# Block copies of the output weights on GpSimd's queue, each transfer tied to a weight split

## The chip, the cores and the metric

The kernel runs on one core of one Trainium2 chip. The metric is the device time of one execution in microseconds (us); lower is better. A core has TensorE (PE, matrix products), VectorE (DVE), ScalarE (ACT) and GpSimd (POOL), each with its own queue of instructions that runs strictly in order, and SyncE (SP), which here only starts transfers. Transfers run on 16 DMA engines that all queues share. A transfer that SP starts goes through hardware queue q1, one that GpSimd starts through software queue q0.

## The reference

One encoder layer on 512 tokens of width 2048, in float32: a normalised, modulated input, one wide input projection, two mixers that read it (dilated-window attention with 16 heads, and gated linear attention, GLA, with 4 heads in both directions), a SiLU gate on each, one output projection, and a normalised residual sum.

```python
mod = jax.nn.silu(c) @ w_cond[layer] + b_cond[layer]
shift, scale, gate = jnp.split(mod, 3, axis=-1)
h = rms_norm(x) * (1.0 + scale[:, None]) + shift[:, None]
proj = h @ w_in[layer]
aq, ak, av, ag, gq, gk, gv, gg, lr_f, lr_b = jnp.split(proj, PROJ_SPLITS, axis=-1)
...
a_out = att.reshape(B, S, ATT_WIDTH) * jax.nn.silu(ag)
...
g_out = g_o * jax.nn.silu(gg)
y = jnp.concatenate([a_out, g_out], axis=-1) @ w_out[layer]
x = x + gate[:, None] * y
return rms_norm(x) * final_gain
```

## The kernel before

**Products.** Each float32 operand is split into a high part (rounded by ScalarE, `split_hi`, L438) and a low part (the difference, by VectorE, `split_lo`, L424), and each product is three TensorE products of such parts (`three`, L215 to L217).

**Stages.** First the modulation (`cb` loads, sums on VectorE) and the first projections (`sta`, `stb`). Then ten units, in this order: qk2, qk4, qk6, gk, gv0, gv1, ag0, ag1, gg0, gg1. A unit (`unit`) makes 512 columns of the projection in eight groups; a group loads 512 KB of weights (`raw`, four buffers, on SP), splits them (three buffers for each part), and does 24 matmuls of 512 columns. At the start of group g the program asks for the split of group g + 1, and it fetches two groups further ahead. Between a unit's matmuls the program puts side work at fractions of its 64 ticks: attention in the first four units, GLA heads in gv1 to gg0, and from qk6 on sums for the gate and the value bias, whose `rawv` and `rawg` loads share the four `raw` buffers and whose work is VectorE's (L314, L839).

**Attention.** For each tile: scores on TensorE (`s`, L726 and L727), a minimum on VectorE (L730), an exponential on ScalarE (L733), a reciprocal on VectorE (`st`, L734), a scaling on GpSimd (`p`, L738), four transposes on TensorE (`t`, L750), a split of the result (`pt`, L754 and L755), and the product with the values (`o`, L764). Between two units the keys of the next four heads are evicted and copied to the other half of the partitions by small SP transfers (`ks`, `kl`). In qk6 the row `srow` and then its spread copy `shb` are also stored and loaded on SP; VectorE's first `rawv` sum needs them. In a GLA head, VectorE's state updates (`st`) take turns with a scaling on GpSimd (`dc`, L926), and `z` (L865) is the head's first product; it needs `lrst` and `ups`, made by VectorE at the start of gv1.

**Output projection.** It is done in two column pairs, each with seven block products in place of eight (`OUT_ORDER`), so some weight operands are sums of blocks: T1 = 11 + 12, T3 = 12 + 22, T2 = T1 + 22, T4 = T2 + 21, four row groups each, for two pairs. That makes 32 sums of 512 KB. Each is made in DRAM, long before the output stage, by two transfers: `sum_start` copies the first block into a DRAM tile (on SP, L393), and `sum_add` adds the second to it in the transfer (on GpSimd, L399). `sum_ops` lists these 64 steps in order, and `SUM_OPS_IN` says how many of them each unit takes; a unit spreads its n steps at fractions (q + 0.5) / n of its ticks.

**Order.** TensorE's order is the program's. On the other engines a scheduler orders the instructions by data dependences and priorities. `tc.issue_after` keeps a transfer behind a named instruction in the order of its own queue: a copy behind SP's last weight load, an addition behind GpSimd's last `p`.

Of the kernel before, what the change touches and what calls it, by code (L numbers as in the profile page):

```python
# [13 lines left out]
AF = mybir.ActivationFunctionType  # L14
ALU = mybir.AluOpType
# [104 lines left out]
OUT_WEIGHTS = {"P1": "11", "P7": "T3", "P6": "T2", "P4": "T4", "P5": "T1", "P3": "22", "P2": "21"}  # L120
OUT_SUMS = {"T1": ("11", "12"), "T3": ("12", "22"), "T2": ("T1", "22"), "T4": ("T2", "21")}
OUT_DEEP = 6
SUM_OPS_IN = {"qk2": 7, "qk4": 7, "qk6": 7, "gk": 7, "gv0": 5, "gv1": 7, "ag0": 7, "ag1": 6, "gg0": 6, "gg1": 5}


def _plan(tasks, free, ready):
# [52 lines left out]
def block_kernel(ctx: ExitStack, tc: tile.TileContext, a: dict):  # L179
    nc = tc.nc  # L180
# [27 lines left out]
    act = nc.scalar.activation  # L208
# [36 lines left out]
    def RAW(name, shape):  # L245
        return wp.tile([P] + shape, F32, tag="raw", bufs=4, name=name)
# [103 lines left out]
    raws, wts, low, last = {}, {}, set(), {}  # L350

    def fetch(i):
        if i < len(groups) and i not in raws:
            u, g = groups[i]
            if u == "O":
                raws[i] = out_fetch(g)
            else:
                raws[i] = RAW(f"raw_{u}{g}", [2, 512])
                last["load"] = nc.sync.dma_start(raws[i], a["w_" + u][g]).ins

    def out_block(pair, which, g):

        l, r = OUT_PAIRS[pair]
        j, z = {"11": (l, g), "21": (l, 4 + g), "12": (r, g), "22": (r, 4 + g)}[which]
        return a[f"w_o{j}"][z]

    def out_fetch(s):

        pair, q = divmod(s, 4 * len(OUT_ORDER))
        what, g = OUT_WEIGHTS[OUT_ORDER[q // 4]], q % 4  # L370
        if s % 2 and s >= OUT_DEEP:
            t = op.tile([P, 2, 512], F32, tag="raw", bufs=3, name=f"raw_O{s}")
        else:
            t = RAW(f"raw_O{s}", [2, 512])
        if what in OUT_SUMS:
            d = dsum[pair, what, g]
            nc.sync.dma_start(t.rearrange("p k c -> p (k c)"),
                              bass.AP(d.tensor, d.offset, [[1024, P], [1, 1024]]))
        else:
            nc.sync.dma_start(t, out_block(pair, what, g))  # L380
        return t

    dsum = {}

    def flat(t):
        return bass.AP(t.tensor, t.offset, [[2048, 64], [1, 2048]])

    def sum_start(pair, name, g):
        def go():
            src = OUT_SUMS[name][0]  # L390
            dsum[pair, name, g] = t = dp.tile([64, 2048], F32, tag=f"{name}{pair}{g}", name=f"{name}{pair}{g}")
            with tc.issue_after(last["load"]):
                nc.sync.dma_start(t, flat(dsum[pair, src, g] if src in OUT_SUMS else out_block(pair, src, g)))  # L393
        return go

    def sum_add(pair, name, g):
        def go():
            with tc.issue_after(last["pool"]) if "pool" in last else nullcontext():
                nc.gpsimd.dma_start(dsum[pair, name, g], flat(out_block(pair, OUT_SUMS[name][1], g)),  # L399
                                    accum_op=ALU.add, max_dma_last_dim=8192)  # L400
        return go

    sum_ops = []
    for s in range(13):
        for lag, fn, name in ((0, sum_start, "T1"), (0, sum_start, "T3"), (1, sum_add, "T1"), (1, sum_add, "T3"),
                              (2, sum_start, "T2"), (3, sum_add, "T2"), (4, sum_start, "T4"), (5, sum_add, "T4")):
            if 0 <= s - lag < 8:
                sum_ops.append(fn(*[((s - lag) // 4), name, (s - lag) % 4]))

    def block_sums(name):  # L410
        n = SUM_OPS_IN[name]
        r = [sum_ops.pop(0) for _ in range(n)]
        return [((q + 0.5) / n, x) for q, x in enumerate(r)]

    def split(i):
        split_hi(i)
        split_lo(i)
# [9 lines left out]
    def split_hi(i):  # L427
        if i < len(groups) and i not in wts:
            fetch(i)
            u, g = groups[i]  # L430
            raw = raws[i].rearrange("p k c -> p (k c)")
            dst = None
            if (u, g) == ("O", len(groups) - gi["O", 0] - 4):
                t = b8.tile([P, 2, 1024], F32R, tag="b8", name="wlast")
                dst = t[:, 0, :], t[:, 1, :]
            wts[i] = dst or (wp.tile([P, 1024], F32R, tag="whi", name=f"{u}{g}h"),
                             wp.tile([P, 1024], F32R, tag="wlo", name=f"{u}{g}l"))
            act(wts[i][0], raw, AF.Copy)  # L438

# [179 lines left out]
    for z in range(2):  # L621
        for e in range(3):
            name = ("mm", "a", 0, 7) if (z, e) == (1, 2) else ("m0", z, e)
# [28 lines left out]
    for w in range(4):  # L652
        for kt in range(4):
            j, g = w // 2 * 4 + kt, w % 2
            task(("vh", j, g), "ACT", 0.42, ["rcol", ("vo", j), ("vl", j - 1, g) if kt else ("hi", 4 * w + 3)],
                 300 - 4 * w - kt, lambda j=j, g=g: v_high(j, g), None if kt else "b8")
            task(("vl", j, g), "DVE", 0.44, [("vh", j, g)], 300 - 4 * w - kt, lambda j=j, g=g: v_low(j, g))
    task(("f", 0), "DMA", 1.5, [("w", "b", KT - 1)], 10, lambda: fetch(0), "raw")
    task(("f", 1), "DMA", 1.5, [("f", 0)], 9, lambda: fetch(1), "raw")
    for i in range(2):  # L660
        task(("s", i), "DVE", 1.3, [("f", i), ("wl", "b", KT - 1)], 850, lambda i=i: split(i), "wts", "raw")
# [341 lines left out]
    def unit(name, natural, side=(), lr=None):  # L1003
# [5 lines left out]
        for g in range(KT // 2):  # L1009
            i0 = gi[name, g]  # L1010
            split_hi(i0)
            split_hi(i0 + 1)
            for ahead in (2, 3):
                fetch(i0 + ahead)
            split_lo(i0)
            hi, lo = wts[i0]
            for i in range(4):
                for kk in range(2):
                    k = 2 * g + kk
                    rh, rl = h_hi[:, k, :], h_lo[:, k, :]  # L1020
                    if natural:
                        t = slice(i * P, i * P + P)
                        cw = slice(kk * 512, kk * 512 + 512)
                        three(ps[i], rh[:, t], rl[:, t], hi[:, cw], lo[:, cw], k == 0, k == KT - 1)
                    else:
                        c = slice(kk * 512 + i * P, kk * 512 + i * P + P)
                        three(ps[i], hi[:, c], lo[:, c], rh, rl, k == 0, k == KT - 1)
                    tick += 1
                    if tick % 8 == 2:
                        split_lo(i0 + 1)  # L1030
                    while pos < len(side) and side[pos][0] * ticks <= tick:
                        urgent(side[pos][1])
                        pos += 1
                if lr is not None:
                    lr(4 * g + i)
# [123 lines left out]
    for e in "hl":  # L1159
        t = hp.tile([P, KT, 512], F32R, tag="h", name="c_" + e)  # L1160
# [263 lines left out]
```

## Time and profile before

| what | us |
|---|---|
| median of 3 runs | 941.84 |
| lowest and highest | 941.41, 942.56 |
| the profiled execution, its time | 948.97 |
| its span, first to last instruction | 947.2 |
| VectorE, ScalarE busy in it | 655.3, 472.8 |
| GpSimd's transfers of sums (L399), median to landing | 7.8 |
| SP's copies from the weights (L393), median to landing | 6.0 |
| rawv loads, rawg loads, median to landing | 4.8, 4.4 |

The times of all rows below the second come from one profiled execution, which took 7.1 us longer than the median. How to read the views that follow: a row of the timeline or of the chain has the start and the length in us, then engine, line, operation and tiles; "x7" after it counts merged instructions, and brackets hold the idle time just before and what ended it. A row of waits has the total in us, the number and the longest. A row of windows has the stretch, its length, the busy time of PE, PEld (weight loads), DVE, ACT and POOL with the number of instructions in parentheses, then the granted TensorE clock, the share of time in which the DMA engines were busy, and GB/s. A queue's row has packets, MB and the share of 16 engines' span.

### The profile page before, as it was taken

To read this page: it belongs to the slowest core of one execution; us is meant where nothing else is said; L and a number is where in the kernel's file an instruction comes from. 1 tells how busy PE (TensorE), PEld (TensorE's weight loads), DVE (VectorE), ACT (ScalarE), POOL (GpSimd) and SP (SyncE) were. 2 spreads that over 40 slices of the span, in tenths; PEclk is the share of its full clock that TensorE was granted. 3 is DMA by queue.
4 is the path that set the end of the run, shared out by engine and by line. 5 is a ranking of instruction groups with operands and counts; after the bars stand their busy time and mean duration, and the time that the engine had idled before them with its cause. 6 is when DMAs were issued, how large, how long until landed. Compare 5 with 4: busy or idle time off the path is not lost.

```text
span 947.2 us, 12118 instructions
## 1 busy us (share of the span) xinstructions
PE 920.3 (97%) x4375; PEld 762.4 (80%) x4375; DVE 655.3 (69%) x960; ACT 472.8 (50%) x770; POOL 84.3 (9%) x120
## 2 busy tenths in 40 slices
PE   8999999999999999999899899999999999999996
PEld 6888888888888878888677688888878888888884
DVE  7988899775756666776333747567697629697486
ACT  5553533655555645555312436354464428555464
POOL 0000000012122122123000010101001000000001
PEclk9999999999999999999899999999999999999998
DMA  9999496654663674954856847566666556866743
GB/s 350 404 411 377 184 374 238 222 156 148 169 203 107 175 260 155 261 177 127 236 156 223 229 157 204 160 218 223 222 217 204 181 153 244 315 210 216 280 176 136
DMA packets 52803, 209.79 MB, mean 221 GB/s; under 512 B 7204, under 2 KB 7492, under 8 KB 45960
## 3 DMA queue, kind: packets, MB, share of 16 engines
q1 hardware_dynamic: 49680, 191.61, 56.5%
q0 software_dynamic: 2624, 16.84, 9.8%
q8 instruction: 34, 0.56, 0.2%
q10 hardware_dynamic: 440, 0.57, 0.2%
q14 instruction: 25, 0.20, 0.1%
HBM read 200.53 MB, written 37.83 MB: 252 GB/s over the span
## 4 chain that ended last, share of the span: by engine, by line
PE 79%; DMA 10%; DVE 5%; issue 3%; ACT 2%; ACTq 0%; DVEq 0%; SPq 0%
DMA rawv<-in_wv 5%; PE ps_qk L215 4%; PE ps_qk L216 4%; PE ps_qk L217 4%; PE g L217 4%; PE g L215 4%; PE g L216 4%; PE stb L217 3%; PE stb L216 3%; PE stb L215 3%; PE ps_ag L217 3%; PE ps_ag L215 3%; PE ps_ag L216 3%; PE t L750 3%; PE o L764 3%
## 5 line engine op out<-in xcount | busy, mean ns | idle before, releaser
L733 ACT ACTIVATE p<-p,st 128x512 f32<-128x512 f32 x64 | 46.1, 720 | 57.7 <-DVE st L730 57.2
L314 DVE CUSTOM_DVE_ANT_0 cb<-cb,sb,c_bcond 128x2048 f32<-128x2048 f32 (+1 forms) x32 | 73.5, 2296 | 0.9 <-DMA cb<-in_wm 0.9
L738 POOL TENSOR_SCALAR p<-p,st 128x512 f32<-128x512 f32 x62 | 44.1, 711 | 327.9 <-DVE st L734 280.1
L730 DVE CUSTOM_DVE_ANT_0 p<-s,g 128x512 f32<-128x512 f32 x64 | 43.7, 688 | 17.8 <-PE s L727 17.2
L755 DVE TENSOR_TENSOR pt<-t,pt 128x512 fp32r<-128x512 f32 x64 | 43.7, 689 | 16.7 <-ACT pt L754 16.2
L399 POOL DMA_DIRECT2D T<-in_w_o x32 | 25.2, 981 | 241.5 <-DMA T<-T 181.4
L754 ACT ACTIVATE pt<-t 128x512 fp32r<-128x512 f32 x64 | 37.9, 592 | 10.7 <-PE t L750 9.7
L764 PEld LDWEIGHTS o<-pt,vv 128*128 128x128 f32 x256 | 35.4, 193 | 7.4 <-DVE pt L755 4.6
L764 PE MATMUL o<-pt,vv 128*128 128x256 f32 x256 | 36.4, 286 | 4.2 <-DVE pt L755 4.2
L750 PEld LDWEIGHTS t<-c_ident,p 128*128 128x128 f32 x256 | 31.8, 141 | 9.9 <-POOL p L738 1.4
L750 PE MATMUL t<-c_ident,p 128*128 128x128 f32 x256 | 39.0, 275 | 0.1
L314 DVE CUSTOM_DVE_ANT_0 rawg<-rawg,sb,gate 128x1024 f32<-128x1024 f32 x16 | 20.5, 1281 | 24.4 <-DMA rawg<-in_wg 24.4
L726 PE MATMUL s<-ks,qs 128*128 128x512 f32 x64 | 25.5, 398 | 1.9 <-DVE pt L755 1.9
L734 DVE RECIPROCAL st<-st 128x1 f32<-128x1 f32 x64 | 10.3, 161 | 24.6 <-ACT p L733 24.5
L314 DVE CUSTOM_DVE_ANT_0 rawg<-rawg,sb,c_bcond 128x1024 f32<-128x1024 f32 x16 | 20.5, 1280 | 7.7 <-DMA rawg<-in_wg 7.7
L727 PE MATMUL s<-kl,qs 128*128 128x512 f32 x64 | 25.2, 394 | 0.0
L314 DVE CUSTOM_DVE_ANT_0 rawv<-rawv,shb,vbias 128x1024 f32<-128x1024 f32 x8 | 10.3, 1282 | 21.3 <-DMA rawv<-in_wv 21.3
L839 DVE CUSTOM_DVE_ANT_0 rawv<-rawv,shb 128x1024 f32<-128x1024 f32 x8 | 9.8, 1223 | 21.0 <-DMA rawv<-in_wv 18.2
L767 ACT ACTIVATE oh<-o 64x256 f32<-64x256 f32 x32 | 12.2, 382 | 19.8 <-PE o L764 19.0
L933 ACT ACTIVATE sq<-st,sc 128x256 f32<-128x256 f32 x24 | 12.2, 507 | 17.4 <-DVE st L928 9.4
L771 DVE TENSOR_TENSOR cat<-o,oh 64x256 f32<-64x256 f32 x32 | 13.3, 416 | 9.1 <-ACT oh L767 8.7
L1249 POOL TENSOR_SCALAR x<-x,rn 128x512 f32<-128x512 f32 x3 | 3.4, 1139 | 178.4 <-ACT rn L1238 178.4
(1519 smaller groups left out, 2973.3 us busy)
## 6 DMA issues: line engine op xcount, KB each, us to landing
cb<-in_wm SPq DMA_DIRECT2D x31, 1024.0 KB, 8.9
T<-in_w_o POOLq DMA_DIRECT2D x32, 512.0 KB, 7.8
rawg<-in_wg SPq DMA_DIRECT2D x32, 512.0 KB, 4.4
raw_O<-T SPq DMA_DIRECT2D x32, 512.0 KB, 4.5
raw_qk<-in_w_qk SPq DMA_DIRECT2D x24, 512.0 KB, 3.4
raw_O<-in_w_o SPq DMA_DIRECT2D x24, 512.0 KB, 4.3
rawb<-in_w_sb SPq DMA_DIRECT2D x16, 512.0 KB, 5.5
T<-in_w_o SPq DMA_DIRECT2D x16, 512.0 KB, 6.0
```

Of the source, the lines that this page charges most:

```text
L215: mm(ps, lh, rh, start=first, stop=False, skip_group_check=more)
L216: mm(ps, ll, rh, start=False, stop=False, skip_group_check=more)
L217: mm(ps, lh, rl, start=False, stop=last, skip_group_check=more)
L314: nc.vector.tensor_tensor_reduce(out=w, in0=w, in1=with_, op0=ALU.mult, op1=ALU.add, scale=1.0, scalar=init, accum_out=dst)
L726: mm(ps, qs[:, q], ks, start=True, stop=False)
L730: nc.vector.tensor_tensor_reduce(out=t, in0=ps, in1=gt[h][:, P * i:P * i + 512], op0=ALU.add, op1=ALU.min, scale=1.0, scalar=3e38, accum_o ...
L733: act(t, t, AF.Exp, bias=st[:, 0:1], scale=-1.0, accum_out=st[:, 1:2])
L738: last["pool"] = nc.gpsimd.tensor_scalar(t, t, st[:, 2:3], 1.0, op0=ALU.mult, op1=ALU.mult).ins
L750: nc.tensor.transpose(pk[:, kt * P:kt * P + P], t[:, kt * P:kt * P + P], ident)
L754: act(hi, src, AF.Copy)
L755: tt(lo, src, hi.bitcast(F32), op=ALU.subtract)
L764: mm(po[:, :256], vv[h // 4][:, kt, h % 4, :], t[:, w, kt, :], start=kt == 0 and w == 0, stop=kt == 3 and w == 1)
```

## The change

`sum_start` no longer uses SP. Both steps go through a new function, `paced`: a GpSimd transfer in pieces of 8 KB that stays behind GpSimd's last `p`, and that also waits, by a semaphore, for the latest weight split that the program has asked of ScalarE. `last["load"]` falls away. The first units take more steps (qk2 and qk4 nine each instead of seven), the units qk6 to gv1 fewer (6, 6, 4, 5 instead of 7, 7, 5, 7), ag1 seven instead of six; the sum stays 64.

```diff
-SUM_OPS_IN = {"qk2": 7, "qk4": 7, "qk6": 7, "gk": 7, "gv0": 5, "gv1": 7, "ag0": 7, "ag1": 6, "gg0": 6, "gg1": 5}
+SUM_OPS_IN = {"qk2": 9, "qk4": 9, "qk6": 6, "gk": 6, "gv0": 4, "gv1": 5, "ag0": 7, "ag1": 7, "gg0": 6, "gg1": 5}
...
-                last["load"] = nc.sync.dma_start(raws[i], a["w_" + u][g]).ins
+                nc.sync.dma_start(raws[i], a["w_" + u][g])
...
+    def paced(dst, src, **how):
+
+        with tc.issue_after(last["pool"]) if "pool" in last else nullcontext():
+            move = nc.gpsimd.dma_start(dst, src, max_dma_last_dim=8192, **how).ins
+        tc.add_manual_dep(move, last["hi"].name, mybir.DependencyInfo(
+            mybir.DependencyClass.Sync, mybir.DependencyReason.DATA), reason="paced")
+
     def sum_start(pair, name, g):
         def go():
             src = OUT_SUMS[name][0]
             dsum[pair, name, g] = t = dp.tile([64, 2048], F32, tag=f"{name}{pair}{g}", name=f"{name}{pair}{g}")
-            with tc.issue_after(last["load"]):
-                nc.sync.dma_start(t, flat(dsum[pair, src, g] if src in OUT_SUMS else out_block(pair, src, g)))
+            paced(t, flat(dsum[pair, src, g] if src in OUT_SUMS else out_block(pair, src, g)))
         return go
 
     def sum_add(pair, name, g):
         def go():
-            with tc.issue_after(last["pool"]) if "pool" in last else nullcontext():
-                nc.gpsimd.dma_start(dsum[pair, name, g], flat(out_block(pair, OUT_SUMS[name][1], g)),
-                                    accum_op=ALU.add, max_dma_last_dim=8192)
+            paced(dsum[pair, name, g], flat(out_block(pair, OUT_SUMS[name][1], g)), accum_op=ALU.add)
         return go
...
-            act(wts[i][0], raw, AF.Copy)
+            last["hi"] = act(wts[i][0], raw, AF.Copy).ins
```

GpSimd's queue at the end of attention, before: the last two p (heads 15) and what follows them. T and three digits is a DRAM sum: name, pair, group; a row from in_w_o with no addition mark can be a copy or an addition, and a second row for the same T is its addition.

```order
L738 TENSOR_SCALAR p150_3963<-p150_3963,st150_3964 128x512
L738 TENSOR_SCALAR p151_4009<-p151_4009,st151_4010 128x512
L399 DMA T110_3148<-in_w_o2 64x2048
L399 DMA T310_3259<-in_w_o2 64x2048
L399 DMA T202_3555<-in_w_o1 64x2048
L399 DMA T400_3709<-in_w_o0 64x2048
L399 DMA T111_3819<-in_w_o2 64x2048
L399 DMA T311_3930<-in_w_o2 64x2048
L399 DMA T203_4208<-in_w_o1 64x2048
```

The same place in the change, with the waits of each:

```order
L742 TENSOR_SCALAR p150_3965<-p150_3965,st150_3966 128x512 [waits DMAHW2_49,DMAHW3_49,DVE_49,PE_49]
L391 DMA T203_4000<-T103_2318 64x2048 [waits DMASW6_49]
L742 TENSOR_SCALAR p151_4013<-p151_4013,st151_4014 128x512 [waits DMAHW4_49,DVE_49,PE_49]
L391 DMA T202_3216<-in_w_o1 64x2048 [waits DMASW7_49]
L391 DMA T401_4214<-T201_2637 64x2048 [waits DMASW0_49,Activation_49]
L391 DMA T400_3446<-in_w_o0 64x2048 [waits DMASW1_49,Activation_49]
L391 DMA T112_4365<-in_w_o3 64x2048 [waits DMASW2_49,Activation_49]
L391 DMA T312_4446<-in_w_o2 64x2048 [waits DMASW3_49,Activation_49]
```

Of the seven additions behind the last p only T202 stays there; those of T110 and T310 have moved ahead into attention, and the transfers behind T202 wait for ScalarE (Activation) as well.

GpSimd's queue in ag0, in the change, around the two directions of one GLA head (dc10 and dc11):

```order
L391 DMA T112_4365<-in_w_o2 64x2048 [waits DMASW4_49,Activation_49]
L930 TENSOR_SCALAR dc101_5121<-st100_5116,sc10_4942 128x256 [waits DVE_49,Pool_49]
L930 TENSOR_SCALAR dc102_5126<-st101_5120,sc10_4942 128x256 [waits DVE_49]
L391 DMA T312_4446<-in_w_o2 64x2048 [waits DMASW5_49,Activation_49]
L930 TENSOR_SCALAR dc111_5169<-st110_5164,sc11_4971 128x256 [waits DVE_49,Activation_49,Pool_49]
```

Before, the transfer at this place was T211's addition, which waited for its copy; now it is T312's, which waits for its copy and for a split of ScalarE.

GpSimd's queue at the end of unit qk4 (the last p of head 7, then the first of head 8), in the change:

```order
L742 TENSOR_SCALAR p72_2691<-p72_2691,st72_2692 128x512 [waits DVE_49]
L391 DMA T200_2263<-in_w_o1 64x2048 [waits DMASW4_49]
L742 TENSOR_SCALAR p73_2733<-p73_2733,st73_2734 128x512 [waits DVE_49,PE_49]
L391 DMA T110_2794<-in_w_o3 64x2048 [waits DMASW3_49]
L391 DMA T310_2893<-in_w_o2 64x2048
L742 TENSOR_SCALAR p80_2913<-p80_2913,st80_2914 128x512 [waits DVE_49,PE_49]
```

Before, the additions of T102 and T302 stood between p73 and p80, and the copy T201 stood on SP ahead of the keys ks of head 8; now two copies stand between the p, one addition ahead of p73, and none of them on SP.

## The prediction

> **What bounds the kernel now.** The page first, for the share of each engine; then TensorE's windows of 25 us, for where the rest is lost.
>
> ```profile
> span 947.2 us, 12118 instructions
> PE 920.3 (97%) x4375; PEld 762.4 (80%) x4375; DVE 655.3 (69%) x960; ACT 472.8 (50%) x770; POOL 84.3 (9%) x120
> ```
> ```profile
> 325.00:350.00 25.00, 23.07 (x109) 18.91 (x108) 15.39 (x35) 10.43 (x21) 4.88 (x7) 0.93 0.80 248
> 450.00:475.00 25.00, 20.77 (x94) 16.92 (x93) 8.18 (x14) 8.17 (x16) 0.00 (x0) 0.86 0.86 226
> 500.00:525.00 25.00, 23.65 (x104) 18.46 (x103) 8.45 (x11) 6.17 (x8) 1.55 (x2) 1.00 0.74 231
> 525.00:550.00 25.00, 21.47 (x91) 17.40 (x90) 19.50 (x23) 14.00 (x25) 0.77 (x1) 0.93 0.64 184
> 825.00:850.00 25.00, 25.00 (x112) 20.71 (x111) 21.20 (x28) 13.25 (x19) 0.00 (x0) 1.00 0.66 230
> ```
> TensorE is full in a window such as the last. So only its few holes can be won, and every new hole is paid in full. TensorE's own waits name the holes:
>
> ```profile
> PE o L764 <- DVE pt L755: 4.2, 1, 4.2
> PE z L865 <- DVE ups L1098: 3.5, 1, 3.5
> PE s L726 <- DVE pt L755: 1.9, 1, 1.9
> PE kt L904 <- DVE ki L894: 1.6, 1, 1.6
> PE ps_gv L217 <- DVE gv06l L424: 1.4, 1, 1.4
> PE ps_gv L217 <- DVE gv05l L424: 0.3, 1, 0.3
> ```
> Together 12.9 us. Behind three of them the granted clock drops (0.93, 0.86, 0.93 above), and TensorE's timeline shows the price at the largest:
>
> ```profile
> 457.90 2.07 PE L764 MATMUL o<-pt,vv 128*128 128x256 f32 x8 [4.20 <-DVE pt L755]
> 459.77 0.63 PE L215 MATMUL ps_gk<-h_hi,gk7h 128*128 128x512 f32 x1
> 462.33 0.45 PE L215 MATMUL ps_gk<-h_hi,gk7h 128*128 128x512 f32 x1
> 463.08 0.40 PE L215 MATMUL ps_gv<-gv00h,h_hi 128*128 128x512 f32 x1
> 463.31 0.39 PE L216 MATMUL ps_gv<-gv00h,h_lo 128*128 128x512 f32 x1
> ```
> Six matmuls from 459.77 to 462.33 start 0.43 us apart instead of 0.23: 1.2 lost, and the eight of L764, half as wide, take 1.87 to the next start instead of 8 x 0.115: 0.9 lost. So 2.1 us there. The windows at 325 and 525 lose 0.07 of the clock where that at 450 loses 0.14; between half of 2.1 and all of it I put 1.5 each. Holes and clock together: 12.9 + 2.1 + 3.0 = 18.0 us, the most that can be won.
>
> **Why the largest hole is there.** GpSimd's queue, and the chain of waits with VectorE's timeline beside it:
>
> ```profile
> 443.81 5.62 POOL L399 DMA_DIRECT2D T<-in_w_o  x7
> ```
> ```profile
> 446.06 9.75 DMA rawv<-in_wv
> 457.27 10.40 DMA rawv<-in_wv
> 470.20 4.20 DMA rawv<-in_wv
> 514.86 9.93 DMA rawg<-in_wg
> ```
> ```profile
> 455.94 1.28 DVE L314 CUSTOM_DVE_ANT_0 rawv<-rawv,shb,vbias 128x1024 f32<-128x1024 f32 x1 [5.23 <-DMA rawv<-in_wv]
> 524.92 1.29 DVE L314 CUSTOM_DVE_ANT_0 rawg<-rawg,sb,gate 128x1024 f32<-128x1024 f32 x1 [10.09 <-DMA rawg<-in_wg]
> ```
> Seven additions leave in one burst at 443.81. The two rawv loads that meet them take 9.75 and 10.40 us, the next one 4.20. VectorE works in order: it sits at the late load, with the pt that TensorE wants queued behind it. In gv0 each rawv load also waits for a buffer that VectorE frees, so the lateness is carried on to gv05l and gv06l.
>
> **The change part by part.** (1) 32 copies leave SP's queue for GpSimd's. No TensorE hole waits for an SP issue, so SP gains nothing that counts. GpSimd pays one issue each, as its additions do:
>
> ```profile
> 273.71 0.70 POOL L738 TENSOR_SCALAR p<-p,st 128x512 f32<-128x512 f32 x1 [1.03 <-DVE st L734]
> 274.35 0.77 POOL L399 DMA_DIRECT2D T<-in_w_o  x1
> 401.09 1.40 POOL L738 TENSOR_SCALAR p<-p,st 128x512 f32<-128x512 f32 x2 [15.12 <-DVE st L734]
> ```
> 32 x 0.77 = 25 us on an engine that is busy 84 us. In the order of the change one transfer at most stands between two p of a unit, in gaps of which the shortest concerned is the 1.03 us above, and pairs stand only at unit ends, in gaps like the 15.12: hidden. Without that cover it would be 0.8 us a time.
>
> (2) The engine time of a copy and of an addition:
>
> ```profile
> q1 hardware_dynamic: 49680, 191.61, 56.5%
> q0 software_dynamic: 2624, 16.84, 9.8%
> ```
> q0 carries the 32 additions: 0.098 x 947.2 = 93 us of all 16 engines, 2.9 us each. At q1's rate (0.565 x 947.2 = 535 us for 191.6 MB) a copy of 0.52 MB is 1.5 us. A copy in 8 KB pieces on q0 is not in this trace: between 1.5 and 2.9; I take 1.5, since it does no addition. So the total load stays, and what counts is whom it meets.
>
> (3) The pace. In the order of the change only one addition (T202) follows the last p that GpSimd does; the next four transfers belong to gv0 and wait for the splits of gv01, gv03, gv05 and gv07, two groups or at least 2 x 24 x 0.23 = 11 us of TensorE work apart. The load of 446.06 then meets one addition instead of seven: 5 to 6 us instead of 9.75, and VectorE is through some 4.5 us sooner. **Hole at 453: 6.3 (4.2 + 2.1); I take 5.5**, bounds 3 and 6.3. **gv05l and gv06l: 1.7; I take 1.5**, bounds 0 and 1.7.
>
> (4) z at 530.75 waits behind the rawg load of 514.86 (9.93 us), which meets two copies and two additions. Now:
>
> ```profile
> 510.61 1.06 ACT L438 ACTIVATE gv11h<-raw_gv 128x1024 fp32r<-128x1024 f32 x1 [7.44 <-PE ps_gv L216]
> 513.61 1.22 DVE L424 TENSOR_TENSOR gv11l<-raw_gv,gv11h 128x1024 fp32r<-128x1024 f32 x1
> ```
> The first addition of gv1 is let go by the end of gv11h, and the rawg load starts when gv11l has freed its buffer: the two still meet, but one to one. Estimate for the load 7 us, and its issue is earlier against TensorE by what gv0 no longer loses. **5.0 (3.5 + 1.5); I take 3.5**, bounds 0 and 5.0.
>
> (5) The hole at 337 (s L726):
>
> ```profile
> 314.51 0.48 SPq L393 DMA_DIRECT2D T<-T  x1
> 314.94 1.59 POOL L399 DMA_DIRECT2D T<-in_w_o  x2
> ```
> ```profile
> 317.66 8.19 DMA ks<-ks
> 325.91 5.93 DMA srow<-shiftt
> 331.90 4.52 DMA shb<-srow
> ```
> ```profile
> 336.45 1.23 DVE L839 CUSTOM_DVE_ANT_0 rawv<-rawv,shb 128x1024 f32<-128x1024 f32 x1 [2.79 <-DMA shb<-srow]
> ```
> A copy and two additions (1.5 + 2 x 2.9 = 7.3 us) lie ahead of ks; srow starts when ks has landed. Now one addition goes out some 4 us earlier, before the last p of qk4, and two copies (3.0) take this place. **3.4 (1.9 + 1.5); I take 3.0**, bounds 0 and 3.4.
>
> (6) kt at 708.5 hangs on a long row of VectorE work, whose order the change shifts by an instruction or two: 1.6 at most either way; I take 0.5.
>
> (7) Against it: at the end of qk2 two additions now leave together after p33, ahead of the next ks. A hole like that of 337 would cost 3.4; the ks and the first score share GpSimd's gap of some 15 us there, so it is mostly hidden: I take 1.0 lost. For GpSimd's new waits 0.5.
>
> **Sum:** 5.5 + 1.5 + 3.5 + 3.0 + 0.5 - 1.5 = 12.5 us of this execution, which took 948.97. The median is 941.84, 7.1 less. If all of that is holes, the median has 11 of the 18 left; if none, all 18. I take the middle, 0.8: 12.5 x 0.8 = 10.0, so **931.8 us**; its own range is 926 to 938.
>
> **Rivals.** *Slower: turn-taking.* A copy on SP's queue waits behind the load ahead of it; on q0 it runs beside the loads, and q0's pieces stretch them, as 9.75 against 4.20 shows. Place: ks at three unit ends, and rawv and rawg in gv0 and gv1, where VectorE has no slack. If two more unit ends become like 337 (6.8), and the five copies of gv0 and gv1 each stretch a load by half of what the burst did (5.55 / 2 x 5 = 13.9), less the burst (6.3), 14.4 us are lost: 956 in full, 949 at half. It decides from where ks takes over 8 us, as at 317.66. For it: q0 is now active about 93 + 48 us. Against it: a copy is half an addition, and additions that met loads singly left no hole in most windows. The Trainium skill, "DMA: Bandwidth & Descriptors" (Queues, rings and completion order), says that each engine goes round robin between queue rows, a packet at a time; by that rule this rival's mechanism is real, and the loads above agree, with its size left to the rows.
>
> *Slower: GpSimd stuck.* It is in order too, and a transfer that waits for a split now stands between two dc:
>
> ```profile
> 602.11 1.04 ACT L438 ACTIVATE ag06h<-raw_ag 128x1024 fp32r<-128x1024 f32 x1
> 606.08 0.48 POOL L926 TENSOR_SCALAR dc<-st,sc 128x256 f32<-128x256 f32 x1 [1.75 <-DVE st L923]
> ```
> ag06h ends at 603.15, plus 0.8 for the issue, and dc comes at 606.08: 2.1 us spare. A split later than that holds dc, VectorE's next st and all splits behind. Five such places at 2 us: 952.
>
> *Half a gain.* Only the burst goes, and the other holes come from VectorE's own loop of load, sum and split: 0.8 x 6.3 = 5.0, 936.8.
>
> *No effect.* In attention the order shows hardly a wait on ScalarE at the transfers, so the pace is not enforced there; gains and new holes cancel: 942.
>
> **How the numbers follow.** Forecast 0.55, half a gain 0.17, no effect 0.08, turn-taking 0.14, stuck 0.06. The range goes from all 18 won (923.8) to turn-taking at a little over a fifth of its price: 924 to 945. Under 0.2% (1.9 us) a measurement here does not tell a change from none: faster 0.74, same 0.07, slower 0.19.
>
> **What would show it.** Right: no run of seven on GpSimd near 444, the rawv loads after 444 under 7 us, no hole at o L764, granted clock 1.00 from 450 to 475. Step 4: rawg ahead of z under 8 us. Step 5: ks at 317 under 6 us. Wrong: a ks or kl over 8 us after qk2 or qk6 with a hole at s; dc waiting for DMA or for a split; p on GpSimd ending after TensorE wants its t.

## The result, and the profile after

| kernel | median, us | lowest to highest | runs |
|---|---|---|---|
| before | 942.89 | 939.03 to 948.34 | 20 |
| changed | 942.64 | 938.62 to 947.34 | 20 |

The ratio is 0.9994, with a 95% interval of 0.9977 to 1.0011: no difference that can be measured. The forecast of 931.8 us was wrong. The profiled execution of the changed kernel took 940.34 us. Its page, with the span, the engines and the two queues:

```profile
span 938.6 us, 12129 instructions
PE 917.5 (98%) x4375; PEld 760.8 (81%) x4375; DVE 654.6 (70%) x960; ACT 472.2 (50%) x770; POOL 98.3 (10%) x152
q1 hardware_dynamic: 48656, 174.83, 51.1%
q0 software_dynamic: 5184, 33.62, 15.1%
```

The copies are on q0 now: it carries twice the bytes, and 0.151 x 938.6 = 142 us of all engines where it had 93. The 49 us more are 1.5 us for each of the 32 copies, as step (2) took.

GpSimd's timeline where the burst of seven additions was, and VectorE's waits for loads in the whole span:

```profile
441.04 0.78 POOL L391 DMA_DIRECT2D T<-in_w_o  x1
447.01 0.53 POOL L391 DMA_DIRECT2D T<-T  x1 [5.19 <-ACT gv01h L442]
461.50 0.77 POOL L391 DMA_DIRECT2D T<-in_w_o  x1 [13.97 <-ACT gv03h L442]
473.36 0.53 POOL L391 DMA_DIRECT2D T<-in_w_o  x1 [11.08 <-ACT gv05h L442]
```
```profile
DVE rawg L314 <- DMA rawg<-in_wg: 50.0, 18, 5.7
DVE rawv L843 <- DMA rawv<-in_wv: 16.0, 7, 6.0
DVE rawv L314 <- DMA rawv<-in_wv: 15.0, 6, 4.6
```

One transfer leaves at a time, and from gv0 on each is let go by a split. No wait for a rawv load is over 6.0 us. From issue to landing the longest rawv load between 444 and 485 takes 5.8 us, the rawg load at 501.5, ahead of the first z, 5.5, and the ks at 318 4.8. TensorE's windows (columns as before) and its largest waits after the first stages show what that brought and what came in its place:

```profile
325.00:350.00 25.00, 25.00 (x129) 20.97 (x128) 16.50 (x37) 12.36 (x25) 6.35 (x9) 1.00 0.72 241
450.00:475.00 25.00, 25.00 (x118) 20.45 (x118) 9.71 (x14) 7.47 (x11) 1.30 (x2) 1.00 0.60 195
525.00:550.00 25.00, 25.00 (x137) 21.54 (x136) 13.77 (x19) 10.26 (x20) 3.25 (x6) 1.00 0.40 128
600.00:625.00 25.00, 22.10 (x112) 18.59 (x111) 13.54 (x20) 12.36 (x17) 2.07 (x3) 0.93 0.67 198
675.00:700.00 25.00, 21.86 (x97) 17.78 (x96) 21.23 (x28) 13.60 (x25) 1.84 (x3) 0.96 0.69 224
```
```profile
PE kt L908 <- DVE ki L898: 3.1, 1, 3.1
PE z L869 <- DVE cat L992: 2.9, 1, 2.9
PE s L730 <- DVE cat L775: 0.2, 1, 0.2
```

The first three windows are full at clock 1.00: the holes at s, o and z that the prediction priced are gone, and every sign that it named for being right is there. All of these signs lie ahead of ag0. The last two, in ag1 and gg0, have new holes. How one of them arises can be read in the chain of waits, in GpSimd's timeline, in VectorE's and in TensorE's:

```profile
603.12 7.43 DMA rawg<-in_wg
610.61 1.18 issue
611.89 5.68 DMA rawg<-in_wg
617.71 1.28 DVE rawg L314
619.00 1.32 DVE cat L992 x2
```
```profile
600.92 0.78 POOL L391 DMA_DIRECT2D T<-in_w_o  x1 [6.70 <-ACT ag10h L442]
610.84 0.53 POOL L391 DMA_DIRECT2D T<-T  x1 [9.15 <-ACT ag11h L442]
```
```profile
610.57 1.28 DVE L314 CUSTOM_DVE_ANT_0 rawg<-rawg,sb,c_bcond 128x1024 f32<-128x1024 f32 x1 [3.19 <-DMA rawg<-in_wg]
617.71 1.28 DVE L314 CUSTOM_DVE_ANT_0 rawg<-rawg,sb,gate 128x1024 f32<-128x1024 f32 x1 [4.70 <-DMA rawg<-in_wg]
```
```profile
616.52 0.39 PE L217 MATMUL ps_ag<-h_lo,ag10h 128*128 128x512 f32 x1
619.81 0.76 PE L869 MATMUL z<-lrst,ups 128*128 128x512 f32 x1 [2.90 <-DVE cat L992]
620.37 0.63 PE L215 MATMUL ps_ag<-h_hi,ag10h 128*128 128x512 f32 x1
620.80 0.63 PE L216 MATMUL ps_ag<-h_hi,ag10l 128*128 128x512 f32 x1
```

Each of the two rawg loads meets a transfer that a split has let go, 2.2 us before the first load and 1.1 before the second. VectorE idles 3.19 and 4.70 us at them, `cat` is queued behind, and TensorE's z waits for `cat`. Behind the hole the matmuls start 0.43 us apart instead of 0.23, so the hole costs more than its 2.90. The hole at kt in gg0 has another shape: the rawg load in its chain takes 4.18 us, as short as the 4.20 of the load that met no burst before.

Where the time went is best read from the start of each unit's first matmul in TensorE's timeline:

| profiled execution | ag0 starts | gg1 starts | ag0 to gg1 | rest |
|---|---|---|---|---|
| before | 577.4 | 741.4 | 164.0 | 205.8 |
| before, a second one | 574.2 | 737.1 | 162.9 | 205.7 |
| changed | 561.1 | 732.8 | 171.7 | 205.8 |
| changed, one from a later run | 560.2 | 736.9 | 176.7 | 205.8 |

The changed kernel reaches ag0 between 13 and 17 us earlier. From there to gg1 it takes 8 to 14 us more than before. How many differs from execution to execution, which fits the spread of the runs over some 9 us.

### The profile page after: what moved, and what is told of

It is laid out like the page before. It is cut to its first block, busy times and chain, and to the rows that moved or that the text cites. A ratio compares the mean times of both kernels' runs of the same rounds, so it can differ in the third digit from the quotient of the medians.

```text
span 938.6 us, 12129 instructions
## 1 busy us (share of the span) xinstructions
PE 917.5 (98%) x4375; PEld 760.8 (81%) x4375; DVE 654.6 (70%) x960; ACT 472.2 (50%) x770; POOL 98.3 (10%) x152
## 4 chain that ended last, share of the span: by engine, by line
PE 81%; DMA 8%; DVE 7%; issue 3%; ACT 1%; POOL 0%; SPq 0%; DVEq 0%; POOLq 0%; ACTq 0%
DMA rawg<-in_wg 5%; PE ps_qk L215 4%; PE ps_qk L217 4%; PE ps_qk L216 4%; PE g L217 4%; PE g L215 4%; PE g L216 4%; PE stb L217 3%; PE stb L216 3%; PE stb L215 3%; PE o L768 3%; PE ps_gv L217 3%; PE ps_gv L216 3%; PE ps_gv L215 3%; PE t L754 3%
## 5 line engine op out<-in xcount | busy, mean ns | idle before, releaser
L391 POOL DMA_DIRECT2D T<-in_w_o x48 | 33.5, 704 | 311.3 <-ACT qk21h L442 119.8
L314 DVE CUSTOM_DVE_ANT_0 rawg<-rawg,sb,gate 128x1024 f32<-128x1024 f32 x16 | 20.5, 1283 | 31.1 <-DMA rawg<-in_wg 30.9
L314 DVE CUSTOM_DVE_ANT_0 rawg<-rawg,sb,c_bcond 128x1024 f32<-128x1024 f32 x16 | 20.5, 1282 | 19.1 <-DMA rawg<-in_wg 19.0
```

The source lines that it names most:

```text
L314: nc.vector.tensor_tensor_reduce(out=w, in0=w, in1=with_, op0=ALU.mult, op1=ALU.add, scale=1.0, scalar=init, accum_out=dst)
L391: move = nc.gpsimd.dma_start(dst, src, max_dma_last_dim=8192, **how).ins
```

## The experiments

All times stand beside runs of the kernel before on the same chip. Ratios are to these, with a 95% interval. The chip differs between experiments, so the ratios compare better than the times.

**The two kernels once more, unchanged.**

> The kernel before, unchanged, profiled once more. Theory 'unlucky profile' (the profiled execution of 948.97 us was a slow draw from a spread of 939 to 948, and its 12.8 us of holes are more than the usual): other or smaller holes than at 337, 453 and 527, together 5 to 9 us, and a profiled time near 942. Theory 'given back' (the change takes these holes away in every execution and makes as many in ag1 and gg0): the same three holes, 11 us or more together, and a gv0 and gv1 of 112 to 114 us together. Ratio to before 1.000 either way.

> The changed kernel, unchanged, profiled once more. 'Given back': holes in front of z (ag1) and of kt (gg0) again, 2.5 to 3.5 us each, and none at s, o or in gv0. 'Unlucky profile': its profile of 940.34 us was a fast draw, so this one shows more holes, 9 us or more, some of them in attention or gv0, and a time near 943.

> The changed kernel, unchanged, timed and profiled once more beside the others of this call. 'No net effect' (the 20 runs so far): ratio 0.998 to 1.002. 'Given back' with a real rest won (its two profiles took 940.3 and 939.9, those of before 949.0 and 944.6): ratio 0.993 to 0.997. Holes in front of z in ag1 and kt in gg0, each 2.5 to 3.5 us, in both cases.

Before: 945.17 us, ratio to itself 0.999 (0.9973 to 1.0006). Changed: one execution at 939.89, and then 942.47, ratio 0.9966 (0.9949 to 0.9984). So the change is worth between nothing and 0.5%, and the bound of a measurement of this kind is about 0.2%. The second trace of before has the same three holes, but smaller: 4.3 us at o, 3.1 at z and 1.5 at s, 8.9 together where 11 or more were expected. The changed kernel's has 3.3 us at z and 2.5 at kt again, and only 0.8 at o. The holes are thus those of the kernels, and not of one execution.

**No sums at all** (the kernel before; the output stage loads a plain block in place of each sum).

```diff
         def go():
-            src = OUT_SUMS[name][0]
...
+            pass
```

> The kernel before without the 64 transfers that make the sums; the output stage loads a plain block where it would load a sum, so the output is not the reference's. It gives the most that any rearrangement of these transfers can win. 'Given back': they cost holes of about 12 us in both kernels, so 930 to 933 us. 'Unlucky profile': holes come mostly from VectorE's own loop of loads and sums, so 937 to 941 us.

930.03 us, ratio 0.9833 (0.9811 to 0.9855). The 64 transfers cost the kernel before some 16 us, and no arrangement tried here won more; the prediction's 18.0 was near it.

**The queue without the pace** (the changed kernel).

```diff
-        tc.add_manual_dep(move, last["hi"].name, mybir.DependencyInfo(
-            mybir.DependencyClass.Sync, mybir.DependencyReason.DATA), reason="paced")
```

> The changed kernel without the wait for the split: copies and additions both on GpSimd's queue in 8 KB pieces, new numbers per unit. 'Given back': if the pace is what empties gv0, a burst on GpSimd behind the last p returns, a hole of 3 to 4 us near 453, and 944 to 950 us. 'Unlucky profile': no difference that can be measured, 941 to 944 us.

969.13 us, ratio 1.0241 (1.0218 to 1.0265). TensorE's waits in it:

```profile
PE ps_gv L217 <- DVE gv04l L426: 8.5, 1, 8.5
PE ps_gv L217 <- DVE gv05l L426: 6.4, 1, 6.4
PE o L766 <- DVE pt L757: 4.8, 1, 4.8
```

When the attention is over nothing holds GpSimd back: it sends one transfer after the other, gv0 takes 76.9 us in place of 52.3, and ag0 to gg0 behind it run as without sums (54.1, 54.1 and 55.3). So without the pace the move of the copies is a plain loss, well above the 944 to 950 us that I expected.

**The same transfers, but small** (the changed kernel; each transfer moves 64 x 32 numbers in place of 64 x 2048, and the output stage loads plain blocks).

```diff
-        return bass.AP(t.tensor, t.offset, [[2048, 64], [1, 2048]])
+        return bass.AP(t.tensor, t.offset, [[2048, 64], [1, 32]])
```

> The changed kernel with the same instructions, waits and order on VectorE, ScalarE and GpSimd, but each of the 64 transfers moves 64 x 32 numbers in place of 64 x 2048, and the output stage loads plain blocks: the sums are left out. If the holes in front of z (ag1) and kt (gg0) come from the bytes that meet the rawg loads, they are gone and the time is that without sums, 930 us (929 to 932). If they come from the other order on VectorE, or from GpSimd waiting for splits, both holes stay and the time is 935 to 940 us.

930.79 us, ratio 0.9849 (0.9827 to 0.9871), as without sums. Behind the first stages TensorE has one wait of note left:

```profile
PE kt L905 <- DVE ki L895: 1.1, 1, 1.1
```

The instructions of the four engines up to the output stage, the waits on GpSimd and the numbers per unit are those of the change. So neither GpSimd's issues nor its waits for splits nor VectorE's order cost anything that can be measured; the holes in ag1 and gg0 come from the bytes.

**Still more steps in the first units** (the changed kernel).

```diff
-SUM_OPS_IN = {"qk2": 9, "qk4": 9, "qk6": 6, "gk": 6, "gv0": 4, "gv1": 5, "ag0": 7, "ag1": 7, "gg0": 6, "gg1": 5}
+SUM_OPS_IN = {"qk2": 11, "qk4": 11, "qk6": 9, "gk": 9, "gv0": 4, "gv1": 4, "ag0": 6, "ag1": 3, "gg0": 2, "gg1": 5}
```

> The changed kernel with other numbers per unit: qk2 11, qk4 11, qk6 9, gk 9, gv0 4, gv1 4, ag0 6, ag1 3, gg0 2, gg1 5; the order on the other engines stays. If the two late holes come from transfers that meet rawg loads, they shrink to under 1 us each and the time is 934 to 938 us, unless the denser transfers of attention make new holes in front of s or o (rival: 942 to 946 us). If they come from VectorE's order, they stay and the time is that of the changed kernel within 2 us.

948.11 us, ratio 1.0028 (1.0009 to 1.0046). TensorE's waits:

```profile
PE ps_gk L215 <- DVE kl L704: 5.5, 1, 5.5
PE kt L908 <- DVE ki L898: 2.7, 2, 2.5
PE s L730 <- DVE pt L759: 2.5, 1, 2.5
PE o L768 <- DVE pt L759: 1.5, 1, 1.5
```

Attention cannot take the transfers of ag1 and gg0: new holes at s, at the start of gk and at o cost more than is won, and the time is above both of the ranges that I expected. Nor is the number of transfers all that counts: with six of them started in ag1 and gg0 instead of 13, kt in gg0 still waits 2.5 us.

**The numbers alone** (the kernel before with the new `SUM_OPS_IN`, copies on SP and additions without a wait).

> The kernel before with the changed numbers per unit and nothing else: copies on SP, additions not paced. If the numbers win the gain in gv0 and gv1, the hole in front of o near 452 is under 2 us and the time 3 to 6 us under before. If it is the pace, GpSimd still sends a burst of additions behind its last p, the hole stays at 3 to 5 us, and the time is within 2 us of before.

938.77 us, ratio 0.9926 (0.9905 to 0.9948): one line of the change does better than the whole of it. The hole at o remains, as GpSimd's timeline and TensorE's waits say:

```profile
439.73 4.82 POOL L399 DMA_DIRECT2D T<-in_w_o  x6
```
```profile
PE o L764 <- DVE pt L755: 4.4, 1, 4.4
```

**Queue and pace with the old numbers** (the fourth corner; the changed kernel with the old `SUM_OPS_IN`).

> Queue and pace of the change with the old numbers per unit: the fourth corner beside the kernel before, the changed kernel and the kernel with the new numbers alone (938.8, 7 us under the kernel before). If the parts add up, queue and pace cost 4 us by themselves: about 949. If the pace does the same work as the numbers at the hole at 453 (it breaks up the burst of additions), the hole at o is gone here too and the time is within 2 us of the changed kernel, so that the loss lies in ag1 and gg0 alone: about 943.

944.27 us, ratio 0.9978 (0.9966 to 0.999). The wait at o falls to 1.2 us in its trace, so queue and pace break the burst up without the numbers; but s waits 3.1 us. Against the kernel before, queue and pace together win next to nothing; against the numbers alone they lose.

**The old way from ag0 on** (the changed kernel; the last 25 steps as before, copies on SP, additions without a wait).

```diff
+        late = len(sum_ops) >= 39
...
-            paced(t, flat(dsum[pair, src, g] if src in OUT_SUMS else out_block(pair, src, g)))
+            if late:
+                with tc.issue_after(last["load"]):
+                    nc.sync.dma_start(t, flat(dsum[pair, src, g] if src in OUT_SUMS else out_block(pair, src, g)))
+            else:
+                paced(t, flat(dsum[pair, src, g] if src in OUT_SUMS else out_block(pair, src, g)))
```

> The changed kernel up to the end of gv1 (39 transfers); the 25 transfers of ag0 to gg1 go the old way, copies on SP behind its last weight load, additions on GpSimd without the wait for a split. Theory A (a paced transfer is let go by the very split that frees the raw buffer for the next rawg load, so transfer and load meet one to one in ag0 to gg1): the change keeps its gain up to gv1 (gv1 starts near 506) and ag1 and gg0 lose their holes at z and kt; ag1 falls from 58.7 us to about 55 and gg0 from 58.9 to about 55.5, so 5 to 8 us under the changed kernel, about 935 where the kernel before is at 943 to 946. Theory C (any 25 transfers in these units cost about the same, whoever starts them): ag1 and gg0 stay within 1.5 us of the changed kernel, and the time too.

934.08 us (932.91 to 934.68), ratio 0.9873 (0.9858 to 0.9888). ag1 and gg0 take 54.1 and 55.5 us in its trace, against 58.7 and 58.9 in the changed kernel's. The same two windows as above, and VectorE's waits from 560 to 760, first here, then in the changed kernel:

```profile
600.00:625.00 25.00, 25.00 (x132) 21.45 (x131) 16.17 (x25) 13.86 (x18) 1.56 (x2) 1.00 0.70 216
675.00:700.00 25.00, 23.76 (x109) 19.43 (x108) 23.11 (x31) 14.95 (x27) 2.87 (x3) 1.00 0.76 227
```
```profile
DVE rawg L314 <- DMA rawg<-in_wg: 20.5, 13, 3.3
```
```profile
DVE rawg L314 <- DMA rawg<-in_wg: 35.3, 15, 5.0
```

The loss of ag1 and gg0 is gone. But the program's numbers per unit are not the numbers that start there: transfers without a wait for a split leave earlier, so that from the first matmul of ag1 to that of gg1 ten start here, as in the kernel before, and 13 in the changed kernel. This run alone does not tell how they are started from how many.

**Copies back on SP throughout** (the changed kernel; the additions keep their wait).

```diff
-            paced(t, flat(dsum[pair, src, g] if src in OUT_SUMS else out_block(pair, src, g)))
+            with tc.issue_after(last["load"]):
+                nc.sync.dma_start(t, flat(dsum[pair, src, g] if src in OUT_SUMS else out_block(pair, src, g)))
```

> The changed kernel with its copies back on SP's queue, behind SP's last weight load; only the 32 additions keep the wait for a split, and the new numbers per unit stay. Theory B (the copies on GpSimd's queue are what costs: there they run beside the loads in place of behind them): about 935, ag1 and gg0 near 55 us each, hole at o gone. Theory A: half of the transfers still leave with the split, so half of the loss stays: ag1 plus gg0 near 114 against 117.6 in the changed kernel and 109.4 without sums; about 938. Theory C: 942.

936.66 us, ratio 0.9888 (0.9862 to 0.9915): between the 935 of the one theory and the 938 of the other. Its trace has one hole of 4.6 us at kt in ag1 and none of note in gg0, so it did not tell the queue of the copies from the pace of the additions. The profiled execution, at 937.93, was the slowest of the four.

**Another trigger** (the changed kernel; from ag0 on the wait is for TensorE's last matmul).

```diff
-        tc.add_manual_dep(move, last["hi"].name, mybir.DependencyInfo(
+        tc.add_manual_dep(move, (tail["mm"] if late else last["hi"]).name, mybir.DependencyInfo(
```

> The changed kernel, but from ag0 on each transfer waits for the last matmul that the program has asked of TensorE instead of for the last split by ScalarE; queue, numbers and order stay. Theory A: the transfers no longer leave with the rawg loads but between them; ag1 and gg0 lose at least half of their excess (8.2 us together over the kernel without sums), the time falls by 3 to 6 us. Theory B (the queue, not the trigger): no change, within 2 us of the changed kernel. A loss would show that the meeting point matters, and that the new one is worse.

941.12 us, ratio 0.9958 (0.9935 to 0.998), as the changed kernel. My idea that the split is a bad trigger, because it also lets the next rawg load go, found no support in this.

**Only the additions free, copies on GpSimd** (the changed kernel; from ag0 on the additions without a wait).

> The changed kernel, but from ag0 on the additions no longer wait for a split; the copies stay on GpSimd's queue with their wait. Theory B2 (from ag0 on it is the copies on GpSimd's queue that meet the rawg loads): no gain, 939 to 943, ag1 plus gg0 at 115 us or more. Theory A2 (the additions' wait for the split is what costs there): as the kernel with the old way from ag0 on, ag1 plus gg0 near 110 us and 934 to 936.

938.71 us, ratio 0.9936 (0.9906 to 0.9966). ag1 is cured in its trace (54.1 us), gg0 is not (59.8): between the two theories, and with runs from 934.24 to 947.26 the widest spread of all.

**Copies on SP, additions paced up to gv1** (new numbers).

> New numbers, all copies on SP's queue, the additions paced up to the end of gv1 and free from ag0 on. Up to gv1 it should run like the kernel with copies on SP (gv0 starts near 453.3 in place of 456.3 in the kernel with the old way from ag0 on); from ag0 on like that kernel (ag1 plus gg0 near 110 us). If both hold, 934.1 less 3: about 931. Theory A2: the hole of 4.6 us at kt in ag1, which the kernel with all additions paced shows, is gone, since its additions there wait no longer. If that hole comes from the phase in which TensorE reaches ag1 (3 us earlier than in the kernel with the old way from ag0 on), it is still there and the time stays at 936.

935.4 us, ratio 0.9884 (0.9859 to 0.9909). The profiled execution has a span of 930.5 us, but the median does not reach the 931 that I expected. This is what the copies look like in SP's timeline, one close behind a weight load, one close behind a rawg load:

```profile
594.13 0.33 SPq L359 DMA_DIRECT2D raw_ag<-in_w_ag  x1
594.55 0.48 SPq L400 DMA_DIRECT2D T<-T  x1
603.73 0.33 SPq L812 DMA_DIRECT2D rawg<-in_wg  x1
604.11 0.48 SPq L400 DMA_DIRECT2D T<-T  x1
```

**What about GpSimd's queue costs?** Three runs. First the copies from ag0 on started by ScalarE, on a hardware queue of their own (else as the kernel just above):

```diff
-            with tc.issue_after(last["load"]):
-                nc.sync.dma_start(t, flat(dsum[pair, src, g] if src in OUT_SUMS else out_block(pair, src, g)))
+            with tc.issue_after(last["hi" if late else "load"]):
+                (nc.scalar if late else nc.sync).dma_start(
+                    t, flat(dsum[pair, src, g] if src in OUT_SUMS else out_block(pair, src, g)))
```

> The kernel of the run before (new numbers, copies on SP, additions paced up to gv1), but the copies of ag0 to gg1 are started by ScalarE, behind the last split that the program asked of it: a hardware queue of their own, still in pieces of 16 KB. Theory L (copies cost little only when they stand in line behind the loads on the loads' own queue; on any other queue they run beside them): VectorE's wait for rawg from 560 to 760 goes back from 21.5 us to 28 or more, ag1 plus gg0 to 113 us or more, the time to 938 to 941. Theory S (it is GpSimd's software queue, whose copies burden the loads, not their running beside them): 934 to 936, the wait at 20 to 23 us.

951.74 us, ratio 1.0053 (1.0032 to 1.0074). TensorE's largest waits and VectorE's from 560 to 760:

```profile
PE kt L919 <- DVE ki L909: 7.6, 3, 4.8
PE z L880 <- DVE cat L1003: 6.9, 1, 6.9
```
```profile
DVE rawg L314 <- DMA rawg<-in_wg: 29.6, 10, 4.9
```

The loss returns, and is far above what I expected. ScalarE never waits for a transfer's end in that stretch, but the issues stand among its activations; how much of the excess is that was not tried. Nor was the size of the pieces on this queue: the trace shows 32 KB for them (not the 16 KB that I wrote), against 8 KB on GpSimd's queue. Second, pieces of 8 KB on SP:

> The kernel of the run before (new numbers, copies on SP, additions paced up to gv1), but the copies on SP go in pieces of 8 KB as in the change. If the size of the pieces were what costs, part of the loss would return (938 to 941, VectorE's wait for rawg from 560 to 760 at 28 us or more). If it is the queue, nothing changes: 934 to 936, the wait at 20 to 23 us.

935.54 us, ratio 0.9889 (0.9862 to 0.9917): on SP's queue the size of the pieces, 8 KB or 32, is not it. (VectorE's wait in the profiled execution was 26.3 us, above the 20 to 23 that were expected.) Third, copies on GpSimd's queue, additions free, and from ag0 on each copy let go by the landing of the last rawg load asked for:

```diff
+            last["rawg"] = nc.sync.dma_start(t[0], a["wg"][m, z]).ins
...
+            paced(t, flat(dsum[pair, src, g] if src in OUT_SUMS else out_block(pair, src, g)),
+                  on="rawg" if late else "hi")
```

> The kernel with copies on GpSimd's queue and additions free from ag0 on (938.7), but from ag0 on each copy waits for the landing of the last rawg load that the program has asked for, in place of a weight split: the moment at which a copy that stands behind that load on SP's queue starts too. Theory M (what counts is the moment: a copy that starts when the load ahead has landed runs while VectorE works on it, one that starts with a split meets the next load): 934 to 937, VectorE's wait for rawg from 560 to 760 at 20 to 24 us, ag1 plus gg0 near 110 us. Theory L (a place in line on the loads' own queue is what counts; on another queue the copy meets a load anyway): 938 to 942, the wait at 27 us or more.

943.39 us, ratio 0.9978 (0.9956 to 1.0001). GpSimd's timeline and VectorE's waits from 560 to 760:

```profile
662.00 0.53 POOL L391 DMA_DIRECT2D T<-T  x1 [8.07 <-DMA rawg<-in_wg]
680.29 0.53 POOL L391 DMA_DIRECT2D T<-T  x1 [11.71 <-DMA rawg<-in_wg]
```
```profile
DVE rawg L314 <- DMA rawg<-in_wg: 30.1, 13, 5.0
```

The copy starts when the rawg load ahead has landed, and VectorE waits for the next one all the same. The moment alone does not save the time, while a copy on the loads' own queue does. All of them side by side (unit lengths, starts of transfers and waits from the profiled executions):

| copies from ag0 on | additions from ag0 on | transfers started in ag1 and gg0 | ag1 + gg0 | VectorE at rawg, 560 to 760 | ratio |
|---|---|---|---|---|---|
| none | none | 0 | 109.4 | 11.1 | 0.9833 |
| SP | free | 10 | 109.6 | 20.5 | 0.9873 |
| SP, copies on SP before ag0 too | free | 10 | 110.2 | 21.5 | 0.9884 |
| the same, 8 KB | free | 10 | 111.1 | 26.3 | 0.9889 |
| SP, copies on SP before ag0 too | paced | 13 | 116.6 | 26.7 | 0.9888 |
| GpSimd, paced | free | 10 | 113.9 | 28.7 | 0.9936 |
| GpSimd, by matmul | by matmul | 13 | 117.2 | 30.8 | 0.9958 |
| GpSimd, on landing | free | 10 | 117.1 | 30.1 | 0.9978 |
| GpSimd, paced (the change) | paced | 13 | 117.6 | 35.3 | 0.9994, 0.9966 |
| ScalarE, copies on SP before ag0 | free | 10 | 125.7 | 29.6 | 1.0053 |

All versions of this table have the new numbers and pace their additions up to gv1 (the first has no sums). Those with copies on SP lie at 0.9873 to 0.9889, and none of their intervals goes above 0.9917; those with them elsewhere lie at 0.9936 or above, and only one of their intervals, that of GpSimd with free additions, begins below 0.9917 (at 0.9906). Among the rows with ten transfers ag1 and gg0 take 109.6 to 111.1 us with the copies on SP and 113.9 or more with them elsewhere, so it is not the number alone that tells them apart. Of the two rows that differ from each other in the copies alone, both with 13, the traces take 116.6 and 117.6 us; there the queue shows only in the medians.

## Why the prediction was wrong, step by step

- **The holes before ag0, steps (3) to (5): right.** The burst is gone, the windows are full, and ag0 starts 13.1 to 16.3 us earlier than in the two traces of before, where the terms up to there add up to 12.0. Against the execution that was priced, 16.3 is nearly all that these holes held. The numbers alone leave the hole at o; queue and pace with the old numbers take most of it away.
- **Step (1), the step that failed.** It moved 32 copies to GpSimd's queue and charged only GpSimd's issues, and step (2) added that the total load stays, so that ag0 to gg1 stood in the sum with no more than kt. The issues are indeed free (small transfers: 930.79). But copies on SP's queue, behind the loads, had a value of their own, which the move gave away: with the new numbers and all additions paced, copies on SP give 0.9888, on GpSimd 0.9966 to 0.9994, some 7 to 10 us. That is most or all of the expected gain. The prediction also did not count that 13 transfers instead of ten start in ag1 and gg0; that costs less, since copies on SP give 0.9888 with 13 there and 0.9873 to 0.9889 with ten. That it was the queue, and not the copies' wait for a split that came with it, is in part argued: no run left them on GpSimd without a wait while the additions kept theirs. Two other waits there, for a matmul (0.9958) and for a landing (0.9978, with free additions), did not bring the time back.
- **Step (2), the copy's engine time: right**, 1.5 us.
- **Step (6), kt: wrong in kind.** I took it for a shift in VectorE's order, worth 0.5. With small transfers, in the same order, kt waits 1.1; with full ones 3.1. So it hangs on the bytes, and a wait for a rawg load stands in its chain.
- **Step (7): too dark.** No hole opened at the end of qk2, though a ks at 251.75 took 8.0 us there, and GpSimd's waits cost nothing.
- **The turn-taking rival blamed the right part of the change and the wrong place.** It put the loss at ks, and at the loads of gv0 and gv1; there nothing was lost. Its loss of 14.4 us in full is near the 8 to 14 lost from ag0 to gg1 by luck, since it is made of other stages. I had set it aside because additions that met loads singly had left no hole; but in those windows no copies ran beside the loads too. Its mechanism, loads stretched by copies beside them, is not shown in ag1 and gg0: from the first matmul of ag1 to that of gg1 a rawg load takes 4.5 us on average in the changed kernel and 4.6 with the old way from ag0 on. The Trainium skill, "DMA: Bandwidth & Descriptors" (Queues, rings and completion order), adds that descriptors of one queue row are taken in ring order while rows take turns; the times fit that, with 935.4 us in line and 943.39 beside, and the loads' own durations do not show it. The Trainium skill, "DMA: Bandwidth & Descriptors" (Issuing engines are not separate DMA queues), says that another issuing engine saves only time on its sequencer; here the runs differ, by 16 us between copies started by SP (935.4) and by ScalarE (951.74), of which an unknown part is due to ScalarE's own order.
- **GpSimd stuck, half a gain, no effect.** No dc waited on a transfer. The time came out where "no effect" put it (942), but not for its reason: the pace was enforced, and a full gain was paid back later.
- **The scaling by 0.8** rested on three runs of 941.41 to 942.56. In all runs since, the kernel before has medians from 942.89 to 946.49 and spreads of 6 to 9 us, so those three were on the low side.

What stays open: the median time of a rawg load from issue to landing between 600 and 740 is 4.4 us in the changed kernel and 4.6 in the one with the old way from ag0 on. So it is not that every load gets slower. It may be which of them is late, and what VectorE has left to do then; no run here separates that further. On GpSimd's queue an addition also stands behind any copy that waits ahead of it, so its additions are never quite free; that was not tried apart either.

**A better version.** New numbers, copies on SP at least from ag0 on, and the additions paced up to gv1: 934.08 and 935.4 us, ratios of 0.9873 and 0.9884. It beats the kernel before by 1.2% and the changed one by about 1%. Of the sums' 16 us it still pays some 4 to 5.

## What to carry to other kernels

A change of several parts is best costed as each part alone: here the new numbers alone were a gain of 0.7%, with paced additions and copies on SP it was 1.1 to 1.2% (intervals that overlap), and the third part, the new queue of the copies, took most of it away. Before a transfer is moved to a queue that looks free, ask which urgent loads it stood in line with, and follow each of them to the end of the program, past the stage that the change aims at. Signs of being right that end where the aimed-at stage ends can all come true while the time stays the same. A full stage with no hole in it is no proof of slack: ag1, which had no hole before, and gg0, which had one of 1.6 us at most, were the ones that broke.

## What the runs showed of the hardware

Ten plain copies of 512 KB started by ScalarE, on another hardware queue than the loads', were dearer than on GpSimd's software queue (ratios of 1.0053 and 0.9936 with the same free additions), though ScalarE was busy only half of the time. How much of that is the queue and how much is ScalarE's order was not tried. And a hole of 2.90 us at z was followed by matmuls at 0.43 us instead of 0.23, so that ag1 took 58.7 us where it needs 54.1 without the sums: the drop of the clock adds more than half of the hole again. The length of a hole does not settle this alone. In the later trace of the same kernel a hole of 2.9 us at z left the clock at 1.00 (window 615 to 625), and around one of 2.7 at kt its mean was 0.79 (window 638 to 646).
